# The substitution of the block inverses and the inverses' read-back, moved behind the queries' rotation

## The chip, the cores and the metric

One Trainium2 chip, one of its cores. The metric is the device time of one launch in microseconds; the times given are medians of several runs. The engines are TensorE (matrix products), VectorE, ScalarE, GpSimd (elementwise work; GpSimd also issues some transfers) and SP, which issues the weight loads. In the profile they are PE (PEld for its weight loads), DVE, ACT, POOL and SP.

## What is computed

Two stacks of two layers on 256 tokens of width 1024, in float32. The second stack's layer is the one that matters here. It projects the normalised tokens, runs three branches (a pooling mixer, a retention branch and an RWKV-7 recurrence), gates and sums them:

```python
def hybrid_layer(x, c_act, positions, ...):
    h = rms_norm_2(x, norm_g) * (1.0 + scale) + shift
    proj = h @ w_in
    pool_u, pool_g, q, k, v, ret_g, rw, rw_g, gate_logits = jnp.split(proj, points, axis=-1)
    o_pool = causal_pool_mixer(pool_u, pool_w, pool_scale) * jax.nn.silu(pool_g)
    o_ret = retention(q, k, v, positions, ret_norm_g) * jax.nn.silu(ret_g)
    o_rwkv = rwkv7_time_mix(rw, ...) * jax.nn.silu(rw_g)
    ...
    return x + gate * (merged @ w_out)

def retention(q, k, v, positions, ret_norm_g):      # rotated queries and keys
    qh = rotary(q.reshape(B, T, H, dh), positions)
    kh = rotary(k.reshape(B, T, H, dh), positions) * (dh ** -0.5)
    ...                                             # decayed scores, times v, head norm

def step(S, inp):                                   # RWKV-7: one token after the other
    r_t, w_t, k_t, v_t, a_t, b_t = inp
    sa = jnp.einsum('bhvk,bhk->bhv', S, a_t)
    S = S * w_t[:, :, None, :] + sa[..., None] * b_t[:, :, None, :] + v_t[..., None] * k_t[:, :, None, :]
    return S, jnp.einsum('bhvk,bhk->bhv', S, r_t)
```

## The kernel before

Float32 products are made of three TensorE matmuls each (lines 138 to 140), from a high part that ScalarE casts (line 112) and a low part that VectorE subtracts (line 113). A weight unit is 128x1024; four raw buffers take the loads, six pairs of buffers the high and low parts, and SP issues the loads in program order, each when a raw buffer is free.

The RWKV recurrence is done in two chunks of 128 tokens and eight heads. Within a chunk it needs the inverse of a unit lower triangular matrix. That inverse is built up from 16x16 diagonal blocks: all 128 of them (two chunks, eight heads, eight blocks) lie one to a partition in `band`, and lines 1504 to 1510 do a forward substitution over 15 rows, two VectorE instructions for each row (a multiply and a sum), each row needing the one before. Their size grows from 1 to 225 elements a partition. The blocks go to a scratch tensor `zd` in device memory (line 1511, issued by GpSimd) and come back in the layout that the products need, as four transfers into `TT[0]` and `TT[1]` (`inverse_parts`, line 1186, also issued by GpSimd). `invert` (line 1188) then extends the inverses to 32 and 64 by products on TensorE.

Around it, in the block that begins at line 1489, TensorE's order is the one that is written there; the order of the other engines' instructions is made by a planner that issues what it takes to be ready, earlier work of the program first. TensorE's order is: the retention values (chunk 5), the bonus, the keys' rotation `rotated(4)`, the queries' rotation `rotated(3)`, half of the gate's product (chunk 6), the retention scores (lines 1389, 1394), the other half of the gate, the retention output (lines 1406, 1409), four steps of the next product (chunk 7), and then the recurrence with the other branches' products between its parts; its first step is `invert`'s product from `TT` (line 1193).

`rotated` handles four parts of 128x256: for each, ScalarE copies the two halves of the product into a `row` buffer (three of them; lines 1373, 1374), GpSimd multiplies it by the sine (1375), VectorE multiplies the product by the cosine (1377), and GpSimd adds the two (1378). The retention norm's statistics are lines 1413 and 1414, its power operation on GpSimd is line 174, and its scaling line 1417.

In the program before, the substitution and the store stand between the two rotations and `inverse_parts` behind the second. Two calls of the planner matter in the change: `tc.issue_after(i)` puts what is written in its block, so far as it runs on the engine of `i`, behind `i` in that engine's order; `tc.keep_in_program_order(i)` puts `i` behind the instruction that was written last before it for the same engine. Both set an order of issue and no wait.

Of the kernel before, what the change touches and what calls it, by code (L numbers as in the profile page):

```python
# [18 lines left out]
AX = mybir.AxisListType  # L19
# [23 lines left out]
def program(ctx: ExitStack, tc: tile.TileContext, T: dict, out: bass.AP):  # L43
    nc = tc.nc
    ver = nc.vector
    act = nc.scalar
    pool = nc.gpsimd
# [10 lines left out]
    def nm(p):  # L58
        uid[0] += 1
        return f"{p}_{uid[0]}"  # L60
# [4 lines left out]
    def bt(tag, shape, dt=F32, bufs=1):  # L65
        p = com if tag in COMMON else blk[0]
        return p.tile(shape, dt, tag=tag, name=nm(tag), bufs={**COMMON, "dg": 2, "TT": 2, "Tn": 2}.get(tag, bufs))

    def st(tag, shape, dt=F32, bufs=3):
        return blk[1].tile(shape, dt, tag=tag, name=nm(tag), bufs=bufs)  # L70

    def pst(tag):
        return ps.tile([128, 512], F32, tag=tag, name=nm(tag), bufs={"mm": 4, "s": 2, "t": 1, "o": 1}[tag])

    def fetch(out, src):
        tc.keep_in_program_order(nc.sync.dma_start(out=out, in_=src))
# [14 lines left out]
    def aux(src, cols=1024):  # L91

        r = bt("gt", [128, 1024])
        fetch(r[:, :cols], src)
        return r
# [46 lines left out]
    def gemm_a(outs, op, units, k0=0, n=512, first=True, last=True, t_outer=False):  # L142
        ks = [(h[:, k, :n], l[:, k, :n]) for h, l, kc in units for k in range(kc)]
        order = [(i, t) for i in range(len(ks)) for t in range(2)]
        if t_outer:
            order.sort(key=lambda a: a[1])
        for i, t in order:
            if outs[t] is None:
                continue
            xh, xl = op.k(k0 + i)  # L150
            s = slice(128 * t, 128 * t + 128)
            mm3(outs[t][:, :n], xh[:, s], xl[:, s], *ks[i], first and i == 0, last and i == len(ks) - 1)

    def gemm_b(o, op, units, col, m=128, k0=0):
        if isinstance(units[0], list):
            units, col = units[col // 256], col % 256
        nk = sum(u[2] for u in units)
        i = 0
        for h, l, kc in units:
            for k in range(kc):  # L160
                xh, xl = op.k(k0 + i)
                mm3(o, h[:, k, col:col + m], l[:, k, col:col + m], xh, xl, i == 0, i == nk - 1)
                i += 1
# [27 lines left out]
    cos = cst.tile([128, 256], F32, name="cos")  # L191
# [10 lines left out]
    def flat2(a):  # L202
        return a.rearrange("p a b -> p (a b)")

    HS = 129 * 128

    def flat(a, off, *ap):
        return bass.AP(tensor=a.tensor, offset=a.offset + off, ap=[list(x) for x in ap])
# [774 lines left out]
    def block2_layer(l, x, r, us, K, xop):  # L983
# [33 lines left out]
        for j in range(4):  # L1017
            if j == (1 if l else 0):
                rb = pst("o")
                for t in range(2):  # L1020
                    dg = flat2(bt("dg", [128, 2, 128]))[:, 0:128]
# [32 lines left out]
        for j in range(0, 8, 2):  # L1054
            u = bt("PT", [128, 2, 256])
            for i in range(2):
                ver.scalar_tensor_tensor(out=u[:, i], in0=rb[:, 0:256], scalar=G[:, j + i:j + i + 1],
                                         in1=x[j // 4][:, j % 4 + i], op0=ALU.mult, op1=ALU.mult)
# [14 lines left out]
        for t in range(2):  # L1073
            p = pst("s")
# [7 lines left out]
        for c2 in range(2):  # L1082
            p = pst("s")
# [11 lines left out]
        p = pst("t")  # L1095
# [12 lines left out]
        for ct in range(4):  # L1108
            p = pst("s")
# [16 lines left out]
        for c2 in range(2):  # L1126
            p = pst("s")
# [5 lines left out]
            for i in range(2):  # L1133
                ct = 2 * c2 + i
                ver.scalar_tensor_tensor(out=Bt[:, ct, :], in0=kT[:, ct, :], scalar=col(57, ct),
                                         in1=p[:, 256 * i:256 * i + 256], op0=ALU.mult, op1=ALU.mult)
# [10 lines left out]
        half = lambda a: slice(64 * a, 64 * a + 64)  # L1147
# [18 lines left out]
        blocks = ([16 * 129, 128], [129, 16], [1, 16])  # L1166
# [11 lines left out]
        band = bt("dg", [128, 16, 16])  # L1178
        pool.dma_start(out=band, in_=flat(K["lt"], 0, *blocks))
        TT = [bt("TT", [128, 8, 64]) for n in range(2)]  # L1180

        def inverse_parts():

            for n in range(2):
                for a in range(2):
                    pool.dma_start(out=TT[n][half(a)], in_=flat(K["zd"], 16 + 8 * HS * n + 64 * 129 * a, [128, 64], [HS, 8], [1, 64]))

        def invert():

# [35 lines left out]
        def bonus():  # L1225

            for n in range(2):
                p = pst("to"[n])
                for ct in range(4):
                    pe.transpose(p[:, 128 * ct:128 * ct + 128], vT[:, ct, tok(n)], ident)  # L1230
                act.copy(out=Vn[:, n, :], in_=p)
            for c2 in range(2):
                p = pst("s")
                for i in range(2):
                    pe.matmul(p[:, 256 * i:256 * i + 256], lhsT=K["bones"], rhs=kT[:, 2 * c2 + i, :],
                              start=True, stop=True)
                ver.tensor_mul(out=flat2(vT[:, 2 * c2:2 * c2 + 2, :]), in0=p, in1=flat2(vT[:, 2 * c2:2 * c2 + 2, :]))
# [113 lines left out]
        def silu_gate(g, c):  # L1351

            us = chunk_b(c)
            for j in range(0, 4, 2):
                p = pst("mm")
                for i in range(2):
                    gemm_b(p[:, 256 * i:256 * i + 256], hop, us, 128 * (j + i))
                    yield
                gv = flat2(g[:, j:j + 2, :])
                act.activation(out=gv, in_=p, func=AF.Tanh, scale=0.5)  # L1360
                ver.scalar_tensor_tensor(out=gv, in0=gv, scalar=1.0, in1=p, op0=ALU.add, op1=ALU.mult)

        def rotated(c):
            us = chunk_b(c)
            dst = bt("gt", [128, 4, 256])
            for j in range(0, 4, 2):
                p = pst("mm")
                for i in range(2):
                    gemm_b(p[:, 256 * i:256 * i + 256], hop, us, 128 * (j + i))
                for i in range(2):  # L1370
                    pi = p[:, 256 * i:256 * i + 256]
                    sw = st("row", [128, 256])
                    act.copy(out=sw[0:64], in_=pi[64:128, :])
                    act.copy(out=sw[64:128], in_=pi[0:64, :])
                    pool.tensor_mul(out=sw, in0=sw, in1=sin)
                    dv = dst[:, j + i, :]
                    ver.tensor_mul(out=dv, in0=pi, in1=cos)
                    pool.tensor_add(out=dv, in0=dv, in1=sw)
            return dst

# [108 lines left out]
        with tc.manual_schedule(engines={mybir.EngineType.PE}):  # L1489
            rv = bt("gt", [128, 2, 512])  # L1490
            us = chunk(5)
            o = [pst("mm"), pst("mm")]
            gemm_a(o, hop, us)
            for t in range(2):
                ver.tensor_copy(out=rv[:, t, :], in_=o[t])
            bonus()
            rk_ = rotated(4)
            pool.tensor_mul(out=Ei, in0=Ei, in1=rT)
            zb = bt("PT", [128, 31, 16])
            pool.memset(zb, 0.0)  # L1500
            pool.memset(zb[:, 15:31, 0:1], 1.0)
            tmp = bt("dg", [128, 256])
            zrow = zb[:, 15:31, :]
            for i in range(14, -1, -1):
                m = 15 - i
                zv = bass.AP(tensor=zrow.tensor, offset=zrow.offset + 16 * i + 15 + 1,
                             ap=[list(zrow.ap[0]), [1, m], [15, m]])
                tv = tmp[:, :m * m].rearrange("p (a b) -> p a b", b=m)
                ver.tensor_mul(out=tv, in0=zv, in1=band[:, i, 1:m + 1].unsqueeze(1).broadcast_to([128, m, m]))
                ver.reduce_sum(out=zrow[:, i, 1:m + 1], in_=tv, axis=AX.X)  # L1510
            pool.dma_start(out=flat(K["zd"], 16, *blocks), in_=zrow)
            rq = rotated(3)
            dm = aux(T["ret_decay"]).rearrange("p (h t) -> p h t", t=256)
            inverse_parts()
            sg[6] = bt("kT", [128, 4, 256])
            gate = silu_gate(sg[6], 6)
            for _ in range(2):
                next(gate)
            scs = retention_scores()
            for _ in gate:  # L1520
                pass
            on = retention_out(*scs)
            others = other_branches(on)
            for _ in range(4):
                next(others)
            for _ in recurrence():
                next(others, None)
            for _ in others:
                pass
# [7 lines left out]
        for c in range(2):  # L1537
# [7 lines left out]
            for j in range(0, 4, 2):  # L1545
                acc = None
                for br in range(3):
                    p = pst("mm")
                    for i in range(2):
                        gemm_b(p[:, 256 * i:256 * i + 256], oop, wb[br], 128 * (j + i), k0=4 * br)  # L1550
                    m = flat2(bt("PT", [128, 4, 128]))
# [18 lines left out]
        for c in range(2):  # L1570
# [5 lines left out]
            for j in range(0, 4, 2):  # L1576
                p = pst("mm")
                sq = bt("PT", [128, 2, 256])
                end = c and j
                for i in range(2):  # L1580
                    xj = x[c][:, j + i]
                    pi = p[:, 256 * i:256 * i + 256]
# [123 lines left out]
    with tc.tile_pool(name="b2", bufs=1) as b2, tc.tile_pool(name="s2", bufs=3) as s2:  # L1706
        blk[:] = b2, s2
        K2 = {}
        xop = unscaled_op(0)
        for j in range(8):  # L1710
            add_unscaled(xop, 0, x, j)
        for l in range(L):
            r, us, xop = block2_layer(l, x, r, us, K2, xop)
        finish(x, r)
# [180 lines left out]
```

## Time and profile before

| | before |
|---|---|
| median of 3 runs | 1619.61 us (1617.99 to 1621.38) |
| profiled execution | 1615.78 us |
| its span, first to last instruction | 1613.7 us |
| mean granted TensorE clock | 0.983 of full speed |
| TensorE, VectorE, ScalarE, GpSimd busy | 96%, 68%, 46%, 16% |

The profile is of one execution; its span is what the timelines count in. "Layer A" and "layer B" below are the first and the second pass of the second stack's layer. A row of a timeline gives the start and the duration in us, the engine, the line of the kernel, the operation, what it writes and reads, how many instructions are merged, and in brackets how long the engine had stood before it and what released it.

### The profile page before, as it was taken

How to read it: one execution, taken by the hardware profiler on the slowest of the kernel's cores; microseconds unless marked ns; L12 is line 12 of the kernel's file. 1: busy time of each engine (PE TensorE's matmuls, PEld its weight loads, DVE VectorE, ACT ScalarE, POOL GpSimd, SP SyncE). 2: the span in 40 equal slices, each digit the busy share in tenths (PEclk: the TensorE clock that was granted, in tenths of full speed). 3: DMA queues.
4: the chain of work that ended last, by engine and by line, in shares of the span. 5: the costliest groups of instructions: out<-in, count | busy, mean ns of one | idle time of the engine just before them, and what ended most of it. 6: DMA issues, size and time to landing. Idle time of an engine off the chain costs nothing.

```text
span 1613.7 us, 29837 instructions
## 1 busy us (share of the span) xinstructions
PE 1549.2 (96%) x12106; PEld 1428.4 (89%) x12106; DVE 1101.8 (68%) x1785; ACT 742.8 (46%) x1194; POOL 260.0 (16%) x255
## 2 busy tenths in 40 slices
PE   7999999899999999998999999899999998999998
PEld 6789997799979899987999888899999988899997
DVE  5576568877676766699876687665565775764754
ACT  4666444444435654454543474433343653433441
POOL 1000110111100000201110142401121422201202
PEclk9899999999999999999999999999999999999999
DMA  8733475587877234664777744544255435443451
GB/s 293 261 106 114 157 231 178 185 280 260 266 250 221 79 105 157 202 220 144 251 270 261 262 141 150 161 148 131 93 181 173 157 102 173 157 133 104 157 184 66
DMA packets 81034, 288.98 MB, mean 179 GB/s; under 512 B 9225, under 2 KB 10305, under 8 KB 80897
## 3 DMA queue, kind: packets, MB, share of 16 engines
q1 hardware_dynamic: 78768, 280.07, 52.3%
q0 software_dynamic: 2128, 7.01, 1.5%
q8 instruction: 95, 1.56, 0.4%
q14 instruction: 43, 0.34, 0.1%
HBM read 281.48 MB, written 5.55 MB: 178 GB/s over the span
## 4 chain that ended last, share of the span: by engine, by line
PE 42%; DVE 6%; DMA 2%; issue 2%; POOL 1%; ACT 1%; DVEq 0%; POOLq 0%; ACTq 0%; SPq 0%
PE mm L138 10%; PE mm L140 10%; PE mm L139 10%; DVE lo L113 2%; PE s L138 2%; PE s L140 2%; PE s L139 2%; DMA zd<-PT 1%; PE s L1159 1%; PE o L1261 1%; PE s L1111 1%; PE t L1261 1%; PE o L1292 1%; ACT hi L112 1%; PE t L1193 1%
## 5 line engine op out<-in xcount | busy, mean ns | idle before, releaser
L113 DVE TENSOR_TENSOR lo<-raw,hi 128x1024 fp32r<-128x1024 f32 (+1 forms) x429 | 545.1, 1278 | 226.0 <-ACT hi L112 224.6
L112 ACT CAST hi<-raw 128x1024 fp32r<-128x1024 f32 (+1 forms) x435 | 453.3, 1048 | 510.8 <-PE mm L139 214.7
L138 PE MATMUL mm<-act,hi 128*128 128x256 f32 x1744 | 504.6, 289 | 7.2 <-ACT hi L112 5.2
L140 PE MATMUL mm<-act,lo 128*128 128x256 f32 x1744 | 496.7, 285 | 3.4 <-DVE lo L113 3.4
L139 PE MATMUL mm<-act,hi 128*128 128x256 f32 x1744 | 495.6, 284 | 0.5 <-DVE act L128 0.5
L138 PEld LDWEIGHTS mm<-act,hi 128*128 128x128 f32 x1744 | 335.6, 192 | 15.4 <-ACT hi L112 5.8
L140 PEld LDWEIGHTS mm<-act,lo 128*128 128x128 f32 x1744 | 335.2, 192 | 5.6 <-DVE lo L113 4.3
L139 PEld LDWEIGHTS mm<-act,hi 128*128 128x128 f32 x1744 | 335.4, 192 | 1.7 <-DVE act L128 0.9
L138 PE MATMUL s<-act,hi 128*128 128x256 f32 x448 | 128.8, 287 | 1.6 <-DVE P L128 1.6
L138 PE MATMUL mm<-hi,act 128*128 128x512 f32 (+1 forms) x320 | 124.8, 390 | 5.6 <-ACT hi L127 5.4
L140 PE MATMUL s<-act,lo 128*128 128x256 f32 x448 | 128.4, 287 | 0.0
L139 PE MATMUL s<-act,hi 128*128 128x256 f32 x448 | 128.4, 287 | 0.0
L140 PE MATMUL mm<-hi,act 128*128 128x512 f32 (+1 forms) x320 | 122.8, 384 | 3.0 <-DVE act L128 3.0
L139 PE MATMUL mm<-lo,act 128*128 128x512 f32 (+1 forms) x320 | 123.3, 385 | 0.8 <-DVE lo L113 0.8
L138 PEld LDWEIGHTS s<-act,hi 128*128 128x128 f32 x448 | 87.8, 196 | 2.4 <-DVE P L128 2.2
L139 PEld LDWEIGHTS s<-act,hi 128*128 128x128 f32 x448 | 87.8, 196 | 0.2
L140 PEld LDWEIGHTS s<-act,lo 128*128 128x128 f32 x448 | 87.7, 196 | 0.0
L1632 DVE CUSTOM_DVE_ANT_0 raw<-raw,gt 128x1024 f32<-128x1024 f32 x48 | 60.8, 1271 | 26.4 <-DMA raw<-in_w_ada 26.3
L138 PEld LDWEIGHTS mm<-hi,act 128*128 128x128 f32 x320 | 60.9, 190 | 18.2 <-ACT hi L127 5.4
L140 PEld LDWEIGHTS mm<-hi,act 128*128 128x128 f32 x320 | 60.7, 190 | 16.5 <-DVE act L128 4.3
L138 PE MATMUL mm<-hi,P 128*128 128x512 f32 x192 | 74.8, 389 | 0.0
L139 PE MATMUL mm<-lo,P 128*128 128x512 f32 x192 | 74.8, 389 | 0.0
(514 smaller groups left out, 2410.0 us busy)
## 6 DMA issues: line engine op xcount, KB each, us to landing
raw<-in_w_in SPq DMA_DIRECT2D x119, 512.0 KB, 4.6
raw<-in_w_up SPq DMA_DIRECT2D x64, 512.0 KB, 4.6
raw<-in_w_down SPq DMA_DIRECT2D x64, 512.0 KB, 4.5
raw<-in_w_gate SPq DMA_DIRECT2D x48, 512.0 KB, 3.4
raw<-in_w_ada SPq DMA_DIRECT2D x48, 512.0 KB, 4.4
raw<-in_w_gl SPq DMA_DIRECT2D x48, 512.0 KB, 3.7
raw<-in_w_branch SPq DMA_DIRECT2D x24, 512.0 KB, 3.4
raw<-in_w_br SPq DMA_DIRECT2D x16, 512.0 KB, 3.3
```

The lines of the kernel that those rows point to most:

```text
L112: act.copy(out=h[:, :cols], in_=r[:, :cols])
L113: (eng or ver).tensor_sub(out=l[:, :cols], in0=r[:, :cols], in1=h.bitcast(F32)[:, :cols])
L138: pe.matmul(o, lhsT=lh, rhs=rh, start=first, stop=False)
L139: pe.matmul(o, lhsT=lh, rhs=rl, start=False, stop=False)
L140: pe.matmul(o, lhsT=ll, rhs=rh, start=False, stop=last)
L1111: pe.matmul(p[:, 256 * n:256 * n + 256], lhsT=ld[n][:, 128 * ct:128 * ct + 128], rhs=K["mcat"], start=True, stop=True)
L1159: pe.matmul(p[par][:, 128 * ct:128 * ct + 128], lhsT=lm[pp, ct, cs], rhs=rm[pp, ct, cs], start=True, stop=True)
L1193: pe.matmul(p[half(a), 64 * i:64 * i + 64], lhsT=lhs(i, a), rhs=rhs(i, a), start=True, stop=True)
L1261: pe.matmul(p[par][:, 64 * ct:64 * ct + 64], lhsT=m[par][:, ct, :], rhs=v(par, ct), start=first and ct == 0, stop=last and ct == 3, skip_g ...
L1292: pe.matmul(p[half(a), col_of(par, ct)], lhsT=TT[n][half(a), 4 * par + ct, :], rhs=x0[half(a), col_of(par, ct)], start=True, stop=True)
L1632: ver.tensor_tensor_reduce(out=r, in0=r, in1=box["c"], scale=1.0, scalar=0.0, op0=ALU.mult, op1=ALU.add, accum_out=mods[l][:, o:o + 1])
```

## The change

The block with the substitution and the store is written behind `rotated(3)` and inside `issue_after` of the last cosine multiply of that rotation, which `rotated` now keeps in `last`. The read-backs of `inverse_parts` are kept in program order on GpSimd. No instruction is added or taken away.

```diff
@@ inverse_parts
-                    pool.dma_start(out=TT[n][half(a)], in_=flat(K["zd"], 16 + 8 * HS * n + 64 * 129 * a, [128, 64], [HS, 8], [1, 64]))
+                    tc.keep_in_program_order(pool.dma_start(
+                        out=TT[n][half(a)], in_=flat(K["zd"], 16 + 8 * HS * n + 64 * 129 * a, [128, 64], [HS, 8], [1, 64])))
...
+        last = []
+
         def rotated(c):
...
-                    ver.tensor_mul(out=dv, in0=pi, in1=cos)
+                    last[:] = [ver.tensor_mul(out=dv, in0=pi, in1=cos).ins]
                     pool.tensor_add(out=dv, in0=dv, in1=sw)
...
             rk_ = rotated(4)
             pool.tensor_mul(out=Ei, in0=Ei, in1=rT)
-            zb = bt("PT", [128, 31, 16])
...
             rq = rotated(3)
+            with tc.issue_after(last[0]):
+                zb = bt("PT", [128, 31, 16])
+                pool.memset(zb, 0.0)
+                pool.memset(zb[:, 15:31, 0:1], 1.0)
+                tmp = bt("dg", [128, 256])
+                zrow = zb[:, 15:31, :]
+                for i in range(14, -1, -1):
...
+                    ver.tensor_mul(out=tv, in0=zv, in1=band[:, i, 1:m + 1].unsqueeze(1).broadcast_to([128, m, m]))
+                    ver.reduce_sum(out=zrow[:, i, 1:m + 1], in_=tv, axis=AX.X)
+                pool.dma_start(out=flat(K["zd"], 16, *blocks), in_=zrow)
             dm = aux(T["ret_decay"]).rearrange("p (h t) -> p h t", t=256)
             inverse_parts()
```

## Rows read from the trace of the kernel before

**Rows 1.** The page, part 1: busy us, share of span, instructions.

```profile
PE 1549.2 (96%) x12106; PEld 1428.4 (89%) x12106; DVE 1101.8 (68%) x1785; ACT 742.8 (46%) x1194; POOL 260.0 (16%) x255
```

**Rows 2.** Waits of TensorE, 1002 to 1105 us: us, times, longest.

```profile
PE mm L1389 <- POOL gt L1378: 4.6, 2, 2.9
```

**Rows 3.** Waits of TensorE, 1339 to 1445 us.

```profile
PE mm L138 <- ACT hi L112: 4.7, 2, 4.1
```

**Rows 4.** Chain of waits, layer A: start us, us, what.

```profile
1023.78 7.42 DMA zd<-PT
...
1042.51 1.22 PE mm L1389 x2
```

**Rows 5.** Timeline of GpSimd, layer A: start, us, instruction, [idle before <- releaser].

```profile
1031.48 0.72 POOL L1186 DMA_DIRECT2D TT<-zd  x1 [6.59 <-DMA zd<-PT]
```

**Rows 6.** Timeline of TensorE, layer A: scores, gate resumed, first product of the inversion.

```profile
1035.76 1.42 PE L1389 MATMUL mm<-gt,gt 128*128 128x256 f32 x4
...
1045.09 0.56 PE L138 MATMUL mm<-act,hi 128*128 128x256 f32 x1
...
1065.63 1.15 PE L1193 MATMUL t<-cpack,TT 64*64 64x64 f32 x32
```

**Rows 7.** Timeline of TensorE, layer B: rotation's end, gate, scores, gate resumed, inversion.

```profile
1364.80 0.28 PE L139 MATMUL mm<-act,hi 128*128 128x256 f32 x1
1364.92 0.28 PE L140 MATMUL mm<-act,lo 128*128 128x256 f32 x1
...
1368.21 0.28 PE L140 MATMUL mm<-act,lo 128*128 128x256 f32 x1
...
1380.84 1.89 PE L1389 MATMUL mm<-gt,gt 128*128 128x256 f32 x8
...
1383.37 0.36 PE L138 MATMUL mm<-act,hi 128*128 128x256 f32 x1
...
1402.91 1.15 PE L1193 MATMUL t<-cpack,TT 64*64 64x64 f32 x32
```

**Rows 8.** Busy us (count) per engine (PE, PEld, DVE, ACT, POOL), clock, DMA, GB/s.

```profile
1042.00:1044.00 2.00, 1.49 (x5) 1.31 (x6) 0.49 (x2) 0.39 (x2) 0.46 (x1) 0.50 0.80 250
```

**Rows 9.** Timeline of VectorE, layer B: substitution sizes 1, 4, 13 and 15.

```profile
1343.51 0.16 DVE L1509 TENSOR_TENSOR dg<-PT,dg 128x1 f32<-128x1 f32 x1 [4.45 <-DMA dg<-lt]
...
1349.10 0.18 DVE L1509 TENSOR_TENSOR dg<-PT,dg 128x16 f32<-128x16 f32 x1
...
1354.68 0.46 DVE L1509 TENSOR_TENSOR dg<-PT,dg 128x169 f32<-128x169 f32 x1
...
1360.04 0.39 DVE L1510 TENSOR_REDUCE PT<-dg 128x15 f32<-128x225 f32 x1
```

**Rows 10.** Timeline of ScalarE, layer A: the copies of the rotation and a cast.

```profile
1028.46 0.37 ACT L1373 COPY row<-mm 64x256 f32<-64x256 f32 x1 [2.65 <-PE mm L140]
...
1029.23 1.05 ACT L112 CAST hi<-raw 128x1024 fp32r<-128x1024 f32 x1
```

**Rows 11.** Groups of VectorE, 1035.6 to 1053 us: busy, mean ns, idle before.

```profile
L113 DVE TENSOR_TENSOR lo<-raw,hi 128x1024 fp32r<-128x1024 f32 x7 | 9.5, 1407 | 2.7 <-ACT hi L112 2.7
```

**Rows 12.** Timeline of VectorE, layer B: low parts behind the scores, first norm statistics.

```profile
1384.30 3.49 DVE L113 TENSOR_TENSOR lo<-raw,hi 128x1024 fp32r<-128x1024 f32 x3
...
1390.30 0.50 DVE L1413 BATCH_NORM_STATS2 rbn<-mm 128x6 f32<-128x128 f32 x2
```

**Rows 13.** Groups of VectorE, 1053 to 1063.1 us: the norm's statistics.

```profile
L1413 DVE BATCH_NORM_STATS2 rbn<-mm 128x6 f32<-128x128 f32 x8 | 2.0, 278 | 0.1
L1414 DVE BATCH_NORM_AGGREGATE rmv<-rbn 128x2 f32<-128x6 f32 x8 | 1.2, 165 | 0.0
```

**Rows 14.** Chain of waits, layer B.

```profile
1361.16 6.38 DMA zd<-PT
...
1377.34 0.21 PE mm L139
```

**Rows 15.** Line 1186, the read-backs: the view's last line.

```profile
DMA to landing us min/median/max: 2.8/3.2/5.2
```

More of the change, by code (lines that the diff above doesn't have):

```diff
@@ L1498, in block2_layer @@
             pool.tensor_mul(out=Ei, in0=Ei, in1=rT)
-            zb = bt("PT", [128, 31, 16])
[L1500 to L1511, printed above, removed]
-            rq = rotated(3)
+            rq = rotated(3)
+            with tc.issue_after(last[0]):
[5 more added lines that the diff above has]
+                for i in range(14, -1, -1):
+                    m = 15 - i
+                    zv = bass.AP(tensor=zrow.tensor, offset=zrow.offset + 16 * i + 15 + 1,
+                                 ap=[list(zrow.ap[0]), [1, m], [15, m]])
+                    tv = tmp[:, :m * m].rearrange("p (a b) -> p a b", b=m)
+                    ver.tensor_mul(out=tv, in0=zv, in1=band[:, i, 1:m + 1].unsqueeze(1).broadcast_to([128, m, m]))
+                    ver.reduce_sum(out=zrow[:, i, 1:m + 1], in_=tv, axis=AX.X)
+                pool.dma_start(out=flat(K["zd"], 16, *blocks), in_=zrow)
             dm = aux(T["ret_decay"]).rearrange("p (h t) -> p h t", t=256)
```

## The prediction

> Throughout, "layer A" is the first pass of the second block's layer (its stretch lies at 1000 to 1070 us) and "layer B" the second (1339 to 1405 us).
>
> **What bounds the kernel now.** I read the page first: TensorE is busy 96% of the span and VectorE 68% [rows 1], so a change pays only where TensorE stands still or runs slowly. Next the waits of TensorE around the change. In layer A it stands 4.6 us for GpSimd's rotation additions [rows 2]; in layer B 4.7 us for ScalarE's casts [rows 3]. The chain of waits says where that begins: GpSimd issues the store to `zd`, the store takes 7.42 us, and only then do the inverses' read-back and the rest of the rotation follow, up to the addition that releases the scores at 1042.51 [rows 4]. GpSimd's own order shows it: the first read-back of `TT` stands in its queue ahead of the rotation's remaining multiplies and waits 6.59 us for `zd` [rows 5]. In layer B the same stop reaches TensorE through ScalarE: its copies wait for the `row` buffers that GpSimd holds, and the cast for the gate's second weight unit stands behind them.
>
> **What the removal is worth (G).** In layer A the scores begin at 1035.76 and the gate resumes at 1045.09, 9.33 us; in layer B, undisturbed, the same work takes 1380.84 to 1383.37, 2.53 us [rows 6, 7]. That is 6.8 us. From there to the first product of the inversion A needs 20.54 us (to 1065.63) and B 19.54 (to 1402.91), because A runs at clock 0.50 for some us after its stop [rows 6 to 8]: 1.0 us. So A can gain 7.8 us and reach the inversion at 1057.8. In B the gate's first half has 36 of its 48 matmuls left at 1368.4 (after the row at 1368.21); at their pitch of 0.12 us that is 4.3 us, so the scores could begin at 1372.7 and not 1380.84: 8.1 us, and the inversion at 1394.8. G is 15.9 us.
>
> **What the move costs.** (1) Substitution, 30 VectorE instructions a layer. In B the steps from size 4 to 12 ran alone from 1349.10 to 1354.68, 5.6 us; the last three sizes take 0.8, 0.9 and 1.3, the first three about 1.1 (rows of 0.16 us with gaps of 0.04). That is 9.7, or 9.3 without one step that ran 0.4 long; I take 9.5 [rows 9]. Before, it ran beside the keys' rotation, where nobody waited for it until 1065.63.
>
> (2) Where it starts now: behind the last rotation multiply on VectorE. The queries' last matmuls end just before ScalarE copies the third part (1028.46); it then casts a weight unit (1029.23, 1.05 us) and copies the fourth (0.75), and the multiply takes 0.42 [rows 10]: 1031.5. In B the matmuls end at 1365.2 [rows 7]; with the same work behind them, 1368.
>
> (3) What lies beside it. In A, between that multiply and the retention norm's statistics, VectorE has seven low parts [rows 11] and four multiplies of 128x512 (three of the scores, one of the gate). At the pitch of an undisturbed run (3.49 us for three low parts, 1.16 each [rows 12]) that is 8.1, and the four multiplies at about 0.6 each give 2.4: 10.5 us. With the substitution's 9.5 this makes 20 us. But the norm's statistics come 9.5 us after the scores' start (B: 1380.84 to 1390.30 [rows 7, 12]), so at 1045.2 in A, under 14 us after the multiply. The substitution can't be done by then, and some of their 3.2 us [rows 13] and the next gate multiply go ahead of it as well. Before, each step waited for its forerunner and ready work slipped between: in B the whole took 1343.51 to 1360.43, 16.9 us for 9.5 us of steps, so 7.4 us of other work came in [rows 9]. I take 3 of at most 4.6 us: the end lies 23 us after the start, 1054.5 in A and 1391 in B. Bounds: 16.5 us, if three of the low parts come ahead of the last rotation multiply, and 24.6, if all the statistics go first.
>
> (4) The way through memory, which was hidden and is now at the end of that chain. About 0.2 us to the issue; the store 6.4 to 7.4; 0.3 to the first read-back; 0.7 for one more issue (the first product needs both halves of `TT[0]`); 2.8 to 5.2 to its landing [rows 4, 5, 14, 15]. Sum 10.4 to 13.8; I take 12, near the middle, since the two rows of the store lie 0.5 to either side of 6.9. So `TT` is there at 1066.5 in A and 1403 in B. TensorE's order is written out by hand, so it waits: 8.7 us in A (against 1057.8) and 8.2 in B (against 1394.8), 16.9 together; bounds 0.1 (16.5 and 10.4) to 12.1 a layer.
>
> The Trainium skill, "DMA: Bandwidth & Descriptors", section on the anatomy of a transfer issued from GpSimd, gives 2.0 us fixed plus bytes at 436 GB/s. By it a 128 KB transfer would take an estimated 2.3 us, and `TT` would be there 6 us after the substitution. The trace does not agree: its stores take 6.4 to 7.4 us.
>
> (5) The clock. After the stops before, it read 0.50 [rows 8]; in B some 27 matmuls behind its stop ran at a pitch of 0.21 and not 0.12 [rows 7, 14], 2.5 us. A stop of 8 us ahead of the inversion should bring it again: I take 2.0 a layer (0 if the wait is short, 2.5 at most), because the products there are small.
>
> (6) With one answer, at no cost: the memsets of `zb` (GpSimd is idle then); the longer life of `zb` in a `PT` buffer (one score tile is all that asks for `PT` before the inversion, and there are four) and of both `dg` buffers (next asked for in the solve, after 1100). Both move with the substitution: the store and four read-backs a layer, 1.1 + 4 x 0.7 us of GpSimd. They pass the rotation's last operations, which is the gain, and the norm's two power operations, which may now queue behind the read-backs: VectorE then waits at the norm's scaling until about 10 us after the store's issue, as late as `TT` itself, so that adds at most 1 us while TensorE waits anyway. SP's weight loads wait for low parts that lie a step or two later; those are cast some 10 us ahead of their matmuls, which covers it.
>
> **Sum.** 15.9 - 16.9 - 4.0 = -5.0: the span goes from 1613.7 to 1618.7, the profiled execution from 1615.8 to 1620.8. The median shown is 1619.6, 3.8 above that execution; on it I forecast 1624.6.
>
> **The rivals.** (a) *The substitution gets through early.* If VectorE takes its steps ahead of the low parts and the score multiplies, it ends near 1046 in A (1031.5 + 9.5, and 5 for what slips in), `TT` lands at 1058, and TensorE hardly waits; delayed low parts may cost 1 to 3 us a layer. Gain 15.9 less 2 to 6: about 1608. It decides from an end before 1045.8 in A (1057.8 - 12). For it: its steps are short and are recorded ahead of that work. Against it: the 16.9 us that they took in B with work between [rows 9].
> (b) *Half and half.* Some low parts come ahead of the last rotation multiply, and the end lies at 18 to 20 us: waits of 4 to 5.5, a gain of 1 to 6 after 2 to 4 for the clock: 1614 to 1619. The same time comes out if store and read-back each land within the quickest row's 2.8 us [rows 15]: `TT` 4.1 + 0.8 us sooner, waits of 3.8 and 3.3, 1614.8 with the clock falling; both rows of the store speak against it, so 3 in 100. The page of the Trainium skill named above, "DMA: Bandwidth & Descriptors", would make this the likely case.
> (c) *Still later.* VectorE also stands in order for casts whose weights land late (2.7 us in A before [rows 11]), and the norm's scaling waits behind the read-backs: waits of 11 to 14 us a layer: 1630 to 1636.
> (d) *It doesn't do what it says*: a rotation operation still stands behind a read-back on GpSimd. It would give 1619.6. Only the steps on VectorE are tied to the rotation, but they take at least 9.5 us, so this is unlikely.
>
> **How the numbers follow.** Chances: forecast 0.46 (1620 to 1629), (a) 0.22, (b) 0.15 with the quick transfers in it, (c) 0.13, (d) 0.04. A measurement can tell about 0.2%, 3.2 us: faster means under 1616.4, slower over 1622.9. Faster: (a) and a third of (b), 0.27. Slower: (c) and three quarters of the forecast, 0.48. Same: 0.25. The range takes in most of (a) and (c): 1608 to 1633. The forecast's own range is 1619 to 1630.
>
> **What would show it.** Right: no wait of TensorE for the rotation's additions and no 4 us wait for the cast; scores at about 1036 and 1373; a new wait at the first product of the inversion, released by `TT`'s transfer; a low clock behind it; the substitution's last step more than 18 us after the last rotation multiply. Wrong: that step within 14 us, and no wait at the inversion; or the rotation still broken by read-backs.

## The result, and the profile after

| | before | after |
|---|---|---|
| median | 1619.61 us (5 runs, 1614.12 to 1621.38) | 1627.88 us (5 runs, 1625.88 to 1630.24) |
| ratio after/before, 95% interval | | 1.0056 (1.0040 to 1.0072) |
| profiled execution, its span | 1615.78, 1613.7 us | 1629.55, 1627.5 us |
| mean granted TensorE clock | 0.983 | 0.978 |

The kernel is slower by 8.3 us, by the medians. TensorE's waits in the two layers come first, as they did ahead of the prediction. The columns are us in total, times, longest. Layer A, 1002 to 1110 us:

```profile
PE t L1194 <- DMA TT<-zd: 8.4, 1, 8.4
PE mm L140 <- DVE lo L113: 1.1, 1, 1.1
PE mm L138 <- ACT hi L112: 0.5, 1, 0.5
```

Layer B, 1339 to 1460 us:

```profile
PE t L1194 <- DMA TT<-zd: 8.2, 2, 8.0
...
PE mm L138 <- ACT hi L112: 0.5, 1, 0.5
```

The waits of [rows 2] and [rows 3] are gone: the scores no longer wait for GpSimd, and of the 4.7 us for casts 0.5 is left. In their place stands one wait at the first product of the inversion, released by the transfer into `TT`. The chain of waits of layer A (start, us, what) says where it comes from, and answers [rows 4]:

```profile
1055.12 0.48 DVE dg L1514
1056.38 7.69 DMA zd<-PT
1064.07 0.29 issue
1064.36 0.71 POOL TT L1186
1065.07 4.54 DMA TT<-zd
1069.65 1.86 PE t L1194 x29
```

VectorE's last large step, the store, the issue of the read-backs, their landing, the product: what was hidden beside the rotation is now the path. GpSimd's timeline of the same stretch (start, duration, line, what, how many, and in brackets the idle time before and its releaser) answers [rows 5]:

```profile
1034.97 1.67 POOL L1381 TENSOR_TENSOR gt<-gt,row 128x256 f32<-128x256 f32 x1
1051.60 1.20 POOL L174 TENSOR_TENSOR rs<-rs,mhalf 128x4 f32<-128x4 f32 x1 [14.96 <-DVE rmv L1417]
1056.38 1.13 POOL L1516 DMA_DIRECT2D zd<-PT  x1 [3.57 <-DVE rbn L1416]
1064.36 2.77 POOL L1186 DMA_DIRECT2D TT<-zd  x4 [6.84 <-DMA zd<-PT]
1067.11 1.07 POOL L174 TENSOR_TENSOR rs<-rs,mhalf 128x4 f32<-128x4 f32 x1
```

The rotation's last addition is issued at 1034.97 without a read-back ahead of it, so the break is gone. The read-backs now wait 6.84 us for the store, and the norm's second power operation stands behind them. VectorE shows what the substitution became: lines 1514 and 1515 are its steps, L1380 the last cosine multiply, L113 low parts, L1416 norm statistics.

```profile
1034.22 0.41 DVE L1380 TENSOR_TENSOR gt<-mm,cos 128x256 f32<-128x256 f32 x1
1034.55 0.35 DVE L1514 TENSOR_TENSOR dg<-PT,dg 128x1 f32<-128x1 f32 x1
1034.83 1.21 DVE L113 TENSOR_TENSOR lo<-raw,hi 128x1024 fp32r<-128x1024 f32 x1
1035.96 0.14 DVE L1515 TENSOR_REDUCE PT<-dg 128x1 f32<-128x1 f32 x1
...
1044.24 1.23 DVE L113 TENSOR_TENSOR lo<-raw,hi 128x1024 fp32r<-128x1024 f32 x1
1045.37 0.23 DVE L1515 TENSOR_REDUCE PT<-dg 128x8 f32<-128x64 f32 x1
...
1055.52 0.28 DVE L1416 BATCH_NORM_STATS2 rbn<-mm 128x6 f32<-128x128 f32 x1
1055.73 0.36 DVE L1515 TENSOR_REDUCE PT<-dg 128x15 f32<-128x225 f32 x1
```

From the multiply's end (1034.63) to the last step's (1056.09) are 21.5 us; in layer B it is 22.7 (1378.25 to 1400.99). Between the steps lie other operations: seven low parts, five multiplies, the norm's first statistics and its first scaling. Last, TensorE at the inversion, and the clock there (stretch; busy us and count of PE, PEld, DVE, ACT, POOL; granted clock; DMA share; GB/s):

```profile
1069.04 2.47 PE L1194 MATMUL t<-cpack,TT 64*64 64x64 f32 x31 [8.38 <-DMA TT<-zd]
...
1071.31 2.01 PE L1194 MATMUL o<-cpack,TT 64*64 64x64 f32 x31
```

```profile
1062.00:1064.00 2.00, 0.00 (x0) 0.00 (x0) 0.00 (x0) 0.00 (x0) 0.00 (x0) 1.00 0.67 100
...
1070.00:1072.00 2.00, 2.00 (x44) 2.00 (x42) 0.00 (x0) 0.35 (x1) 0.00 (x0) 0.50 0.00 0
...
1074.00:1076.00 2.00, 2.00 (x16) 2.00 (x15) 2.00 (x8) 0.13 (x1) 0.00 (x0) 0.84 0.00 0
```

TensorE stood still, then ran at 0.50 of full speed, 1.2 and not 2.4 GHz, until about 1074.6. 31 of its second group of products take 2.0 us, against 1.15 for 32 in [rows 6].

**Where the time went, row by row.** TensorE's matmuls stand in the same order in all kernels here, so each can be set against the same one in the trace of before, and the difference of their starts followed along the span. For the changed kernel (us later than before; minus is earlier):

```
                       layer A                      layer B
before the rotations   +2.4  (before's 1003 us)     +9.2  (1340 us)
retention output       -5.0  (1052)                 +2.8  (1393)
first inversion row    +3.4  (1066)                +10.9  (1403)
behind the inversion   +6.3  (1127)                +13.8  (1480)
```

Within the layers it gains 7.4 and 6.4 us up to the retention output, then loses 8.4 and 8.1 to the wait and 2.9 and 2.9 behind it: 3.9 and 4.6, together 8.5 us, close to the 8.3 between the medians. The spans of the two profiled executions differ by more, 13.8. The other 5.3 us lie where nothing moved, as between 1335 and 1340 us, where the granted clock was 0.50 in after and 1.00 in before. Profiled executions of the kernels below vary by -4 to +11 us in such stretches. So causes are read from the two layers alone, and effects from medians and ratios.

Of the 2.9 us behind the wait, some 0.4 is a second, short pause: the later transfers into `TT` land behind the first. Layer B shows it:

```profile
1413.81 0.47 PE L1194 MATMUL t<-cpack,TT 64*64 64x64 f32 x2 [8.01 <-DMA TT<-zd]
1414.49 1.86 PE L1194 MATMUL t<-cpack,TT 64*64 64x64 f32 x29 [0.21 <-DMA TT<-zd]
```

The third product starts 0.52 us behind the second there and 0.45 in layer A, and the others start 0.1 apart. So 2.5 us a layer are left for the slow clock.

### The profile page after: what moved, and what is told of

The parts are those of the page before. It is cut to its first block, busy times and chain, and to the rows that moved or that the text cites. A ratio compares the mean times of both kernels' runs of the same rounds, so it can differ in the third digit from the quotient of the medians.

```text
span 1627.5 us, 29837 instructions
## 1 busy us (share of the span) xinstructions
PE 1554.4 (96%) x12106; PEld 1434.2 (88%) x12106; DVE 1094.9 (67%) x1785; ACT 742.4 (46%) x1194; POOL 260.6 (16%) x255
## 4 chain that ended last, share of the span: by engine, by line
PE 44%; DVE 5%; DMA 2%; issue 2%; ACT 1%; POOL 1%; DVEq 0%; POOLq 0%; ACTq 0%
PE mm L138 10%; PE mm L140 10%; PE mm L139 10%; DVE lo L113 2%; PE s L138 2%; PE s L139 2%; PE s L140 2%; PE s L1159 1%; DMA zd<-PT 1%; ACT hi L112 1%; PE o L1262 1%; PE s L1111 1%; PE t L1194 1%; PE o L1194 1%; PE t L1262 1%
## 5 line engine op out<-in xcount | busy, mean ns | idle before, releaser
L113 DVE TENSOR_TENSOR lo<-raw,hi 128x1024 fp32r<-128x1024 f32 (+1 forms) x429 | 543.1, 1272 | 232.0 <-ACT hi L112 229.3
```

Source lines behind the costliest of these rows:

```text
L113: (eng or ver).tensor_sub(out=l[:, :cols], in0=r[:, :cols], in1=h.bitcast(F32)[:, :cols])
```

## The experiments

Each ran beside the kernel before on one chip; a ratio is to that kernel's runs, with its 95% interval. Four chips were used, and on them the kernel before took 1617.0 to 1620.8 us, so two changed kernels are compared by their ratios and not by their medians. "Local" is the sum over both layers of the differences just described, from one profiled execution each. The columns give, for each layer, the difference up to the retention output, and from there to behind the inversion.

```
                         layer A        layer B       local   median   ratio (interval)
after                  -7.4 +11.3     -6.4 +11.0      +8.5   1627.9   1.0056 (1.0040-1.0072)
changed again          -7.4 +11.3     -7.8 +11.8      +7.9   1628.0   1.0043 (1.0027-1.0058)
move alone             -7.4 +11.2     -7.8 +11.5      +7.4   1626.4   1.0057 (1.0037-1.0078)
pin alone              -7.4  +1.2     -7.4  +0.0     -13.6   1604.6   0.9935 (0.9914-0.9955)
pin alone again        -7.4  +1.3     -5.5  +0.0     -11.5   1605.0   0.9926 (0.9903-0.9948)
no substitution wait   -7.4  +0.0     -7.8  +0.0     -15.2   1605.6   0.9933 (0.9916-0.9950)
no power wait          -7.4  +9.3     -7.8 +11.3      +5.3   1629.9   1.0088 (1.0066-1.0110)
half way               -5.6  +5.9     -3.4  +0.0      -3.0   1615.4   0.9994 (0.9979-1.0010)
eight rows             -7.4  +1.6     -7.8  +2.1     -11.6   1604.5   0.9940 (0.9912-0.9968)
eleven rows            -7.4  +6.8     -7.9  +7.7      -0.8   1619.2   1.0001 (0.9981-1.0021)
store by rows          -7.4  +9.6     -6.4  +9.4      +5.3   1623.2   1.0031 (1.0013-1.0049)
fill, 32 matmuls       -7.4 +13.8     -7.8 +13.8     +12.4   1634.3   1.0075 (1.0051-1.0098)
fill, 18 matmuls       -7.4  +9.0     -7.8  +9.0      +2.7   1623.7   1.0036 (1.0021-1.0051)
```

The theory: the rotation's break was worth some 15 us, and the loss is TensorE's wait for a chain that begins when the substitution ends, with a slow clock behind it. The main rivals: the pin itself costs; the load on VectorE costs; the read-backs' place in GpSimd's queue costs; the transfers are held by something else.

### The two parts of the change, one at a time

The move alone (the pin is taken off):

```diff
-                    tc.keep_in_program_order(pool.dma_start(
-                        out=TT[n][half(a)], in_=flat(K["zd"], 16 + 8 * HS * n + 64 * 129 * a, [128, 64], [HS, 8], [1, 64])))
+                    pool.dma_start(out=TT[n][half(a)], in_=flat(K["zd"], 16 + 8 * HS * n + 64 * 129 * a, [128, 64], [HS, 8], [1, 64]))
```

> Only the move: the substitution and the store behind the queries' rotation as in the changed kernel, the read-backs without the pin. Since the substitution ends some 20 us behind the rotation, the read-backs come behind it by themselves. Theory (the pin is without effect beside the move): as the changed kernel, 1624 to 1630, with a wait of TensorE of 8 us at the first inversion product in both layers. Rival (the pin costs, since it holds something behind the transfers): 1616 to 1622.

Measured: 1626.4 us, ratio 1.0057, and TensorE's wait at the inversion 8.2 and 8.9 us. The pin is without effect beside the move. The pin alone is the kernel before with only the other part:

```diff
-                    pool.dma_start(out=TT[n][half(a)], in_=flat(K["zd"], 16 + 8 * HS * n + 64 * 129 * a, [128, 64], [HS, 8], [1, 64]))
+                    tc.keep_in_program_order(pool.dma_start(
+                        out=TT[n][half(a)], in_=flat(K["zd"], 16 + 8 * HS * n + 64 * 129 * a, [128, 64], [HS, 8], [1, 64])))
```

> Only the pin: the substitution stays between the two rotations, and GpSimd's read-backs are kept behind the rotation's last operation. Theory (the gain comes from the rotation no longer being broken by the read-backs, the loss from the substitution's late start and its way through memory): the break goes (15.9 us by the working of the prediction, less up to 4 for the stores' issue on GpSimd and other work that falls in), the inverses are in TT at about 1042 and 1378, well ahead of 1058 and 1395, so no wait of TensorE at the inversion: 1604 to 1608, with no read-back in GpSimd's order ahead of a rotation operation. Rival 1 (the break was not worth that: the work that TensorE then reaches earlier waits for weights or casts instead): 1612 to 1620, the waits reappearing within 30 us of the rotation. Rival 2 (the pin is what costs, since it holds the norm's power operations or the loads behind the transfers): 1620 to 1628.

> The pin alone once more, beside the shorter fill, on the same chip: 1602 to 1608, no wait of TensorE at the inversion.

Measured: 1604.6 and 1605.0 us, ratios 0.9935 and 0.9926: 12 us less than the kernel before beside it, and by the ratios some 19 us less than the changed kernel. GpSimd's timeline of layer A shows the order that does it:

```profile
1032.14 1.12 POOL L1512 DMA_DIRECT2D zd<-PT  x1
1033.26 0.77 POOL L1376 TENSOR_TENSOR row<-row,sin 128x256 f32<-128x256 f32 x1
...
1040.62 1.61 POOL L1379 TENSOR_TENSOR gt<-gt,row 128x256 f32<-128x256 f32 x1
1042.17 2.77 POOL L1186 DMA_DIRECT2D TT<-zd  x4
```

The store goes out ahead of the queries' rotation, its landing lies beside the rotation, and the read-backs wait for nothing when their turn comes, behind the last addition. No wait for `TT` is left. What stays of the layer's loss is a wait for the gate's multiply on VectorE:

```profile
PE mm L138 <- DVE kT L1362: 1.0, 1, 1.0
```

So either part alone takes the break away: up to the retention output the move gains 7.4 and 7.8 us, the pin 7.4 and 5.5 to 7.4. Behind it the pin costs 0.0 to 1.3 us a layer, and the move 11.2 to 11.5.

### What the inversion waits for

First the changed kernel with read-backs that do not depend on the moved work:

```diff
-                    tc.keep_in_program_order(pool.dma_start(
-                        out=TT[n][half(a)], in_=flat(K["zd"], 16 + 8 * HS * n + 64 * 129 * a, [128, 64], [HS, 8], [1, 64])))
+                    pool.dma_start(out=TT[n][half(a)], in_=flat(K["lt"], 16 + 8 * HS * n + 64 * 129 * a, [128, 64], [HS, 8], [1, 64]))
```

> The substitution and its store stay moved as in the changed kernel, but the inverses are read back from the scratch tensor lt, which was complete before, and not from zd; so the read-backs wait for nothing that is moved, and the inverses are other numbers. VectorE does the same instructions as in the changed kernel, at the same place. Theory (the loss is TensorE's 8 us wait at the first inversion product, and the slow clock behind it): that wait goes in both layers, the other waits stay gone, 1603 to 1609. Rival (the loss is the load on VectorE, whose low parts and score multiplies come later because the substitution lies between them): 1620 to 1628, with waits of TensorE for low parts in its place.

Measured: 1605.6 us, ratio 0.9933. VectorE does the same steps at the same place, and TensorE loses nothing behind the retention output, in either layer (+0.0, +0.0). The rival of VectorE's load falls. The gain within the layers, 7.4 and 7.8 us, is the price of the break. The ratio is worth less, 8 to 14 us, than the local 15.2. The rest lies outside the two layers and stays open.

Then the substitution cut short, first to eight rows:

```diff
-                for i in range(14, -1, -1):
+                for i in range(14, 6, -1):
```

> The changed kernel with the last seven of the substitution's 15 rows left out (sizes 9 to 15; the inverses are not complete). In the changed kernel's trace the eighth size's sum ends at 1045.6 in layer A and 1390.2 in layer B, 10.5 us ahead of the last one. Theory (TensorE's wait follows the end of the substitution, one for one, through a transfer chain of constant length): the inverses arrive 10.5 us sooner, ahead of the end of TensorE's own work, so no wait, and no slow clock: 1603 to 1608. Rival (the transfers are held by something else, such as the weight loads that share the DMA engines): a wait of over 3 us stays, 1614 to 1622.

Measured: 1604.5 us, ratio 0.9940. The wait for `TT` is down to 1.2 us in layer A and none in B (where 1.0 us is a wait for the norm's scaling), so it follows the substitution's end. But the chain was longer than expected; the chain of waits of layer A:

```profile
1042.82 8.53 DMA zd<-PT
1051.64 0.71 POOL TT L1186
1052.35 6.66 DMA TT<-zd
```

Store and landing take 8.53 and 6.66 us here, against 7.69 and 4.54 in the changed kernel, with the same bytes. "A transfer chain of constant length" was wrong. With eleven rows (`range(14, 3, -1)`):

> The changed kernel with the last four of the 15 rows left out (sizes 12 to 15). In the changed kernel's trace the eleventh size's sum ends at 1050.4 and 1395.3, 5.5 us ahead of the last one. Theory (as for eight rows): a wait of 8.2 less 5.5, about 2.7 us, stays in each layer. In the changed kernel's trace the granted clock fell some 3.5 us into the wait, so it should not fall here: 1604 and 5.4 give 1608 to 1612. Rival (any stop there brings the slow clock, 2.8 us a layer): 1613 to 1617.

Measured: 1619.2 us, ratio 1.0001. The theory's 1608 to 1612 is missed, and so is the rival's 1613 to 1617, although the rival's mechanism came. TensorE at the inversion, and the clock:

```profile
1060.74 2.31 PE L1194 MATMUL t<-cpack,TT 64*64 64x64 f32 x31 [3.96 <-DMA TT<-zd]
```

```profile
1060.00:1062.00 2.00, 1.26 (x18) 1.10 (x19) 0.00 (x0) 0.00 (x0) 0.00 (x0) 0.50 0.45 80
...
1066.00:1068.00 2.00, 2.00 (x18) 2.00 (x18) 1.50 (x5) 0.00 (x0) 0.00 (x0) 0.93 0.00 0
```

Two things fail. The wait is 4.0 us (4.3 in layer B) and not 2.7, since the landing took 6.58 us. And a stop of 4 us brings the slow clock as one of 8.4 does (0.86 already in 1058 to 1060, and 0.50 from there): 6.8 less 4.0 is 2.8 us behind it in layer A, 7.7 less 4.3 is 3.4 in B. Less the pauses for the later transfers (0.2 and 0.8), 2.6 is left in each, against 2.5 after the long stop.

Last, the store in longer runs, one of 1024 bytes for each partition in place of 16 of 64:

```diff
-                pool.dma_start(out=flat(K["zd"], 16, *blocks), in_=zrow)
+                pool.dma_start(out=flat(K["zd"], 16, [16 * 129, 128], [16, 16], [1, 16]), in_=zrow)
```

> The changed kernel with the store to zd written as one run of 1024 bytes for each partition in place of 16 runs of 64 bytes (the same bytes, other places, so that the read-backs find other numbers). Theory 1 (the 7 to 7.7 us of the store are the price of its 2048 short runs): it lands in 2.5 to 4 us, the wait of TensorE falls from 8.3 to about 4.5 us, the clock falls late or not at all: 1613 to 1619. Theory 2 (the store's time is a fixed price of a transfer that is issued on GpSimd, or queueing behind weight loads): it stays at 6 to 7.7 us and the time at 1625 to 1629.

Measured: 1623.2 us, ratio 1.0031; the median lies between the two theories. The store was as the first theory had it, the time was not. The chain of waits, and TensorE at the products:

```profile
1054.94 2.06 DMA zd<-PT
...
1059.36 7.62 DMA TT<-zd
```

```profile
1063.33 0.47 PE L1194 MATMUL t<-cpack,TT 64*64 64x64 f32 x2 [4.12 <-DMA TT<-zd]
1064.37 1.96 PE L1194 MATMUL t<-cpack,TT 64*64 64x64 f32 x30 [0.56 <-DMA TT<-zd]
```

```profile
1070.00:1072.00 2.00, 2.00 (x12) 2.00 (x11) 2.00 (x7) 0.00 (x0) 0.00 (x0) 0.50 0.00 0
1072.00:1074.00 2.00, 2.00 (x14) 2.00 (x14) 1.90 (x2) 0.00 (x0) 0.00 (x0) 0.73 0.17 45
```

The same 128 KB land in 2.06 us as 128 runs and in 7.69 as 2048. Only the runs, and with them the places in `zd`, differ: the store's price is its short runs. Of the 5.6 us saved, the wait shows 3.7 (8.4 to 4.1 and 0.6), because the read-backs took 5.2 to 7.7 us to land and not 3.6 to 4.6. The DMA share behind their issue is 0.98 to 1.07 (1060 to 1064), against 0.83 and 0.94 in the changed kernel (1064 to 1068). The clock fell again, and TensorE worked at 0.50 for longer: from 1063.3 to about 1073, where the changed kernel has 1069 to 1074.6. Behind the first product 5.4 and 6.2 us are lost; less the pauses for the later transfers (1.4 and 2.3), the slow clock costs 4.0 and 3.9 us and not 2.5. So it takes back about half of what the shorter waits and pauses save (3.2 and 3.0).

### Half way

The substitution between the rotations, as before, but tied behind the keys' last cosine multiply on VectorE; read-backs pinned.

```diff
             rk_ = rotated(4)
             pool.tensor_mul(out=Ei, in0=Ei, in1=rT)
-            rq = rotated(3)
             with tc.issue_after(last[0]):
...
+            rq = rotated(3)
```

> The substitution and its store are written between the two rotations, as before the change, but behind the last cosine multiply of the keys' rotation on VectorE; the read-backs are pinned as in the changed kernel. Theory (what decides is when the substitution begins, not that it is moved nor the pin): it begins at about 1022 and 1358, ends before 1040 and 1376, the inverses are there 12 us later, before 1058 and 1395, and TensorE does not wait for them: 1604 to 1612, the higher end if the store, which stands in GpSimd's order among the queries' rotation, holds its last two parts until the substitution is done (2 to 4 us a layer). Rival (any start behind the keys' rotation is too late, since ready work slips between the steps): a wait of 2 to 5 us at the inversion, 1614 to 1622.

Measured: 1615.4 us, ratio 0.9994, no difference. There is no wait for `TT`, so the rival's mechanism is wrong, but the theory's time is missed too. TensorE's waits of layer A and two rows of VectorE:

```profile
PE mm L138 <- DVE kT L1362: 4.0, 1, 4.0
PE mm L140 <- DVE lo L113: 3.6, 2, 3.1
```

```profile
1032.99 0.39 DVE L1514 TENSOR_REDUCE PT<-dg 128x15 f32<-128x225 f32 x1
1033.29 1.22 DVE L113 TENSOR_TENSOR lo<-raw,hi 128x1024 fp32r<-128x1024 f32 x1
```

Here the substitution ran almost alone, 1022.44 to 1033.38: 10.9 us with two cosine multiplies of 0.4 in it. The low parts that were pushed behind it came late, and TensorE waited 3.6 us for them and 4.0 for the gate. The gate's wait goes through the weights: the cast that ScalarE does ahead of the gate stood 2.5 us for a load. That this load was late because the low parts freed its buffer late is argued, not shown. The store held GpSimd 2.0 us as expected. A substitution that goes first charges the low parts; one that goes last charges the inversion.

### The norm's power operation, and the clock

```diff
-                                      scalar2=rs[:, h:h + 1], op0=ALU.subtract, op1=ALU.mult)
+                                      scalar2=mhalf[:, h:h + 1], op0=ALU.subtract, op1=ALU.mult)
```

> The changed kernel, but the retention norm's scaling multiplies by a constant instead of by the inverse deviation, so it no longer waits for GpSimd's power operation (which still runs). The output of the retention branch is other numbers. Theory (TensorE's wait is for the transfers, and VectorE's waits of 8.1 and 8.6 us at the norm's scaling, behind the read-backs in GpSimd's order, lie beside it): VectorE's wait goes, TensorE's wait at the inversion stays 8 us, 1625 to 1628. Rival (the read-backs' place ahead of the norm's power operation is what delays what follows): 1616 to 1621.

Measured: 1629.9 us, ratio 1.0088. VectorE's waits at the norm, 8.1 and 8.6 us in the changed kernel, are gone, TensorE's at the inversion are still 7.5 and 8.4, and the time is no shorter, so the rival falls. Within layer A the loss behind the retention output is 2.0 us smaller (9.3 against 11.3), within B it is as before. That the time is above the changed kernel's is not explained by the layers (+5.3 local): the profiled execution loses 4.2 us already ahead of 900 us, where the two kernels do the same, and a granted clock of 0.974 to 0.979 runs through its executions. This stays open.

For the clock, the changed kernel with matmuls of two constants ahead of the inversion:

```diff
+            fill = pst("mm")
+            for _ in range(32):
+                pe.matmul(fill[:, 0:256], lhsT=ident, rhs=cos, start=True, stop=True)
             for _ in recurrence():
```

> The changed kernel with 32 matmuls of 128x128 by 128x256 added on TensorE ahead of the inversion's first product, in both layers; they read two constants and write a PSUM buffer that nobody reads. At the scores' pitch of 0.23 us they take 7.4 us, so they fill most of the 8.2 us in which TensorE stands there, and end before the inverses arrive. Theory (behind the stop the slow clock costs 2.8 us a layer, which a busy TensorE would not lose): the granted clock stays at 1.00 behind the stop, the products take 1.1 us in place of 1.9, and the time falls by about 5.7 us against the changed kernel, to 1621 to 1624. Rival (what is lost behind the stop is lost to casts and low parts that came late, not to the clock): no gain, 1626 to 1630.

> The changed kernel once more, beside the one with the filled stop, on the same chip: 1625 to 1630, a wait of 8 us at the inversion's first product in both layers and a granted clock of 0.50 behind it.

Measured: 1634.3 us against 1628.0. The size was wrong: the trace records each of these float32 matmuls as two, and the 32 took 14.0 us. Their 13.8 us in the table are all there is: behind them the clock is 1.00 and nothing is lost. With 18:

> As the kernel with the filled stop, with 18 matmuls in place of 32: there each ran as two passes, 0.436 us a matmul and 14.0 us in all, 5.6 us longer than the stop of 8.3. 18 take 7.9 us. Theory (the loss behind the stop, 2.6 to 2.9 us a layer, is the slow clock's): the inversion's products begin when the inverses land, as in the changed kernel, at granted clock 1.00, and nothing is lost behind them: against the changed kernel 5.4 us less, 1620 to 1624. Rival (behind the stop it is lost to late casts and low parts): 1626 to 1630.

```profile
1060.86 7.93 PE L1532 MATMUL mm<-cos,cpack 128*128 128x256 f32 x36
1069.25 0.33 PE L1194 MATMUL t<-cpack,TT 64*64 64x64 f32 x2 [0.46 <-DMA TT<-zd]
...
1070.85 1.15 PE L1194 MATMUL o<-cpack,TT 64*64 64x64 f32 x31
```

Measured: 1623.7 us. The second group of products takes 1.15 us in place of 2.0. The loss behind the retention output falls from 11.3 and 11.8 us (the changed kernel, again) to 9.0 in each layer, by 5.1 together. Of these, 1.0 is inverses that came sooner (the first product is 8.3 and 8.5 us late, against 8.7 and 9.1). Behind the first product the loss falls from 2.6 and 2.8 us to 0.6 in each layer. The pauses for the later transfers are 0.3 and 0.4 of the former and 0.5 and 0.4 of the latter. So the slow clock costs 2.3 and 2.4 us, and with the stop filled at most 0.2 is left for anything else, late casts included. The times do not show it alone: the ratios, 1.0036 here and 1.0043 to 1.0057 for the changed kernel and the move alone, have intervals that overlap, and the median came from another chip.

## Why the prediction was right, point by point

The forecast was 1624.6 us by a loss of 5.0; measured were 8.3. Its steps:

**G, the break of the rotation.** Put at 7.8 and 8.1 us. Measured up to the retention output: 7.4 and 6.4 in the changed kernel, 7.4 and 7.8 with the read-backs freed. Right, and a little too large.

**(1) to (3), the substitution's end.** Its steps alone: 9.5 put, about 10.1 shown half way (10.9 less two multiplies of 0.4). From multiply to end: 23 put, 21.5 and 22.7 measured. The reading of [rows 9], that ready work slips between the steps, held, and the seven low parts of the estimate are the seven in the trace. The fifth multiply is the "next gate multiply" of the estimate. What it did not name, the norm's first scaling, took the room of statistics that came behind the last step. The "at most 4.6" is not the sum of what is named beside it: 3.2 for the statistics and 0.6 for that multiply are 3.8, and the upper bound would be 23.8. Rival (a) needed the opposite, and the runs show both sides of it: with eight rows the end comes early and the time falls to 1604.5; where the steps did run through, half way, the low parts and the gate paid, in layer A more than the 1 to 3 us that it allowed (5.9).

**(4) The way through memory.** Put at 12 of 10.4 to 13.8 us; measured 12.9 and 12.8 (1056.09 to 1069.04, 1400.99 to 1413.81). TensorE's waits: 8.7 and 8.2 put, 8.4 and 8.2 measured. That they fit so closely is in part luck: the substitution was 1.5 and 0.3 us shorter than put, the way through memory 0.9 and 0.8 longer. The store took 7.7 us, more than either row of before, and the read-backs 3.6 to 4.6. The Trainium skill, "DMA: Bandwidth & Descriptors", section on the anatomy of a transfer issued from GpSimd, has a formula in bytes alone; the estimate by it is 2.3 us for 128 KB. With 128 runs of 1024 bytes the trace agrees (2.06); with 2048 runs of 64 it does not (6.1 to 9.5). So the quick-transfer case of rival (b) did exist, but needed another layout. Even then the time was 1623.2, not 1614.8, since the read-backs lengthened and the slow clock cost 4.0 and 3.9 us, where 2.0 a layer were put. The Trainium skill, same page, section on queues, rings and completion order, says that a DMA engine takes turns between the queues that have work for it. That fits read-backs that slow down beside weight loads; no run here separates it from a limit of the memory.

**(5) The clock.** This term was mis-sized: 2.0 us a layer put, "because the products there are small", with 2.5 as the most. The changed kernel's rows show 2.9 in each layer behind the first product, of which 2.5 is the clock's; against the filled stop it is 2.3 and 2.4. TensorE works at 0.50 for some 5.2 us (1069 to 1074.6, less the pause), on the products and then on the matmuls of the next weights, and half of that is 2.6. The pauses for the later transfers, 0.4 a layer, were not in the sum. Within the layers the loss was 3.5 us larger than the forecast's (8.5 against 5.0): the smaller G is 2.1 of it, the clock 1.0, the pauses 0.8, and the waits were 0.4 shorter. In the changed kernel again it was 2.9 larger, with G 0.7 of it, the clock and the pauses 0.7 each, and longer waits 0.9. So the clock and the pauses are short in both, and the rest varies between executions.

**(6) At no cost.** The norm's power operation did queue behind the read-backs, for 8 us, and without that wait the time was no shorter; the 2.0 us in layer A of that run are the most that one execution shows for it, where 1 was put. The waits of TensorE, VectorE, ScalarE and GpSimd show none for `zb` or the `dg` buffers, and TensorE waits for no weight load there.

Rival (c) named the same mechanism with a longer chain, and (d) fell with the rotation's waits. The rows named as signs all came: no wait for the rotation's additions, the new wait released by `TT`, the low clock, a last step more than 18 us behind the multiply. The scores came at 1038.5, and 1383.7, which is 1036.1 and 1374.5 without the 2.4 and 9.2 us that the run was late ahead of them.

One thing the prediction did not ask: which of the change's two parts does what. The rows for it were there. [rows 5] showed that the read-back's place in GpSimd's queue was the break, and [rows 9] that the substitution was done in time. The pin alone follows from these two, and by the ratios it is the better kernel by some 19 us (0.9935 and 0.9926 against 1.0056 and 1.0043).

## What to carry to other kernels

Here a transfer that waited at the head of an engine's queue was cured best by moving the waiting instruction back in that queue, and not the work that it waits for: pin the read-back, and leave the producer early. Before moving a producer, add up its whole way to the consumer, steps with what slips between them, store, issue, landing, against the time until the consumer is reached, and leave room for landings that vary. A stop of TensorE had a second price behind it, and a shorter stop did not make it smaller: 2.6 us behind one of 4.0, 2.5 behind one of 8.4, 4.0 behind one of 4.1 (layer A). In all three it was about half of the time that TensorE worked at half speed, 5.3, 5.2 and 8.3 us.

## What was not expected of the hardware

The same 128 KB stored to device memory took 2.06 us as 128 runs of 1024 bytes, and 6.1 to 9.5 us over the other kernels as 2048 runs of 64 bytes. The read-backs' landing from `zd` ran from 2.8 to 9.2 us over the kernels, with equal bytes and layout; what else the DMA engines carried is the likely reason, but no run separates it. The slow clock cost as much after a stop of 4.0 us as after one of 8.4 (2.6 and 2.5 us in layer A), and more after one of 4.1 with the store in longer runs (4.0).
